# Attention inside a hybrid encoder layer: transposes, rounding and products with v one unit later

## The chip, the cores and the metric

The kernel runs on one core of a Trainium2 chip. Its engines work side by side, each through its own list of instructions in order: TensorE (PE in the profile; PEld is its weight load, which overlaps), VectorE (DVE), ScalarE (ACT), GpSimd (POOL) and SyncE (SP), of which the last two here mainly issue DMAs. Instructions of different engines wait for each other through semaphores. TensorE writes its results to PSUM, which the kernel uses as eight banks of 128 x 512 float32 values; a bank is taken, filled by TensorE, read by VectorE or ScalarE, and given back.

The metric is the device time of one launch in microseconds, as the median of several runs; less is better.

## What is computed

One layer: an RMS norm, one projection `w_in`, softmax attention in 16 heads of 64 beside gated linear attention in 4 heads, one projection `w_out`, then an RMS norm and a gated feed-forward part. There are 512 tokens, 2048 features, all in float32. The change lies in the softmax attention:

```python
def dilated_window_attention(q, k, v, rel_table, window, dilation):
    ...
    logits = (jnp.einsum('bhrnqd,bhrnkd->bhrnqk', qb, kb).astype(jnp.float32)
              * (Dh ** -0.5) + bias[None, :, None, None])
    logits = jnp.where(valid[None, None, None], logits, -1e30)
    m = jnp.max(logits, axis=-1, keepdims=True)
    p = jnp.exp(logits - m)
    s = jnp.sum(p, axis=-1, keepdims=True)
    o = jnp.einsum('bhrnqk,bhrnkd->bhrnqd', p, vb.astype(jnp.float32)) / s
...
def mixture_of_dilations(q, k, v, rel_table):
    for window, dilation in DILATION_PATTERNS:
        o, l = dilated_window_attention(q, k, v, rel_table, window, dilation)
    ...
    w = jax.nn.softmax(jnp.stack(lses, axis=0), axis=0)
    out = sum(w[i][..., None] * outs[i] for i in range(len(outs)))
```

The kernel folds the three dilation patterns into one table of biases per head and computes one softmax over 512 keys.

## The kernel before

**Precision.** TensorE's fast float32 form rounds its inputs. Each operand is therefore split into a rounded part and what is left over ("hi" and "lo"), and a product takes three matmuls (hi x hi, hi x lo, lo x hi), or two where one side needs no split. Rounding is a ScalarE copy, the rest a VectorE subtraction; both show in the profile under their lines (L237 and L218 for streamed weights, L671 and L677 for the softmax).

**Jobs.** Between about 400 and 750 us TensorE works through jobs of dense matmuls, each run by `run_job` (L308): gqk, gv0 and gv1 (projections for the gated attention), then out(1), out(2), ... for `w_out`. A job fills four banks; its inner loop issues groups of three matmuls (L346 to L348), one group for each bank and slice of rows. At its end the four banks are emptied by the job's evacuation: L836 and L839 on VectorE for gqk, L861 on ScalarE for gv0 and gv1, L1298 on VectorE for the out jobs. The banks go back one by one to a list from which the next `ps.get()` takes the one that was given back first.

**Side work.** Between two groups, `run_job` adds a quarter of the job's rate to a credit, 3.1 for gqk and the gv jobs and 4.0 for the out jobs. For every whole credit `run_side` takes one step from the front of a list of urgent generators (if there is one) and one from the front of the side list: the low-rank gate, then `attention()`, then the `silu` gates and `gla`, the gated attention with four heads in `turns`. A generator's step reaches to its next `yield`. All order on the engines follows from these lists, and the engines' instructions stand in the order in which the Python code issues them.

**Attention.** It has 64 units: 16 heads times 4 blocks of 128 queries. A step of `attention()` (L720 on) handles several units at different stages and has two halves with a `yield` behind each. In step u before the change:

- first half: scores of unit u on TensorE (`att_scores`, L631 and L632, into a bank); scale of unit u - 2 (`att_scale`, L658, ScalarE, odd units only); exp of u - 1 (`att_exp`, L649, ScalarE); rounding of u - 3 (`att_round`, L671, ScalarE); in even steps the lift (`att_lift`, L697, ScalarE) of a pair of units;
- second half: transposes of u - 2 (`att_transpose`, L663, TensorE, into a bank); in odd steps the products with v (`att_av`, L687 and L688, TensorE, into a bank); then on VectorE the rest of u - 3 (`att_rest`, L677, which frees the transposes' bank), the maximum with bias of u (`att_max`, L641, which frees the scores' bank), in even steps the mix of a pair (`att_mix`, L706, which frees the products' bank), and the reciprocal of the sum of u - 1 (`att_norm`, L652), with the normalisation of even units right behind it (L654).

Scaling by the reciprocal thus falls to ScalarE for odd units and to VectorE for even ones. The job holds four banks, attention has the other four.

**What feeds it.** q and k of a pair of heads are read back from memory by `read_qk` (L569, DMAs on GpSimd) in steps with u % 8 == 2 and rounded by `load_qk` (L588 on VectorE, L592 on ScalarE, five stages) which is put into the urgent list in steps with u % 8 == 5, so that one stage is issued ahead of each half step. `load_bias` (L552, a DMA on SyncE) reads the bias tables of two heads ahead at the first block of a head; `load_v` reads the second half of v in steps 33 to 35.

**Gated attention.** `gla` issues its gates, a scan (L950) and its tables (L962 to L981, VectorE, with exp on ScalarE between), then some empty half steps, and then transposes of keys (L1016) and products (L1019), each into a bank of its own, which `copy_predicated` (L1022) and a copy (L1026) empty. Head 0 has one more empty half step than the others.

Of the kernel before, what the change touches and what calls it, by code (L numbers as in the profile page):

```python
# [27 lines left out]
NH = 16  # L28
# [84 lines left out]
def put(*slots):  # L113
    for s in slots:
        if s.home is not None:
            s.home.free.append(s.i)


def layer(nc, tc, x, attn_norm_w, w_in, rel_table, gw_f, gb_f, gw_b, gb_b, gla_norm_w, w_out,
# [7 lines left out]
    with tc.manual_schedule(), \  # L127
# [134 lines left out]
        urgent = deque()  # L262

        def run_urgent():
            while urgent:
                try:
                    next(urgent[0])
                    break
                except StopIteration:
                    urgent.popleft()  # L270
# [277 lines left out]
        def load_bias(h):  # L548
            if h < NH and h not in biast:
                biast[h] = s4.get(F32, [P, BIASW])  # L550
                src = bass.AP(tensor=line.tensor, offset=line.offset + h * LINE, ap=[[1, P], [1, BIASW]])
                sp.dma_start(out=biast[h].t, in_=src)  # L552
# [18 lines left out]
        def load_qk(pr):  # L571


            qs, ks = qkr.pop(pr)
            sign = (-1.0, 1.0)[pr % 2]
            QK[pr] = []
            v = lambda x_: x_.rearrange("p (b c) -> p b c", c=P)
            low = slice(64, 128)
            todo = []
            for n in range(2):  # L580
                e, k = s2.get(F32R), s2.get(F32R)
                todo += [(v(e.t), v(e.f), v(qs[n].f)[:, :, ::-1], v(e.t)[low], -sign * DH ** -0.5, low, qs[n]),
                         (k.t, k.f, ks[n].f, ks[n].t, sign, slice(0, 128), None)]
                QK[pr].append((e, k, ks[n]))
            for m in range(5):
                if m:
                    _, hf, src, lo, scale, r, done = todo[m - 1]
                    dve.scalar_tensor_tensor(lo, src[r], scale, hf[r], op0=OP.mult, op1=OP.subtract)  # L588
                    if done:
                        put(done)  # L590
                if m < 4:
                    act.activation(todo[m][0], todo[m][2], AF.Copy, scale=todo[m][4])  # L592
                    yield
            ready.add(pr)

        def load_v(half, ts=range(4)):
            for t in ts:
                v = s4.get(F32R, [P, 8, 2, DH])
                VS.setdefault(half, []).append(v)
                sp.dma_start(out=v.f.rearrange("p h s c -> p (h s c)"), in_=vd[4 * half + t])  # L600
# [20 lines left out]
        UNITS = 4 * NH  # L621

        def att_scores(u):
            h, b = divmod(u, 4)
            q, k, kl = QK[h // 2][h % 2]
            c = slice(b * P, (b + 1) * P)
            if b == 0:
                load_bias(h)
                load_bias(h + 1)
            s = ps.get()  # L630
            mm(s.t, q.t[:, c], k.t, start=True, stop=False)  # L631
            mm(s.t, q.t[:, c], kl.t, start=False, stop=True)  # L632
            if b == 3:
                put(q, k, kl)
            AT[u] = s
# [77 lines left out]
        def attention():  # L713


            def run(f, u, n=UNITS):
                if 0 <= u < n:
                    f(u)

            for u in range(UNITS + 6):  # L720
                h = u // 4
                if u < UNITS:
                    if u % 8 == 2:
                        read_qk(h // 2 + 1)
                    if u % 8 == 5 and h // 2 + 1 < NH // 2:
                        urgent.append(load_qk(h // 2 + 1))
                    while h // 2 not in ready:
                        run_urgent()
                if "mix" in at:
                    pr = at.pop("mix")  # L730
                    mixh[pr] = split_of(mixf.pop(pr), big=pr > 4)
                run(att_scores, u)
                run(att_scale, u - 2)
                run(att_exp, u - 1)
                run(att_round, u - 3)
                if u % 2 == 0:
                    run(att_lift, (u - 6) // 2, UNITS // 2)
                yield
                run(att_transpose, u - 2)
                if u % 2:  # L740
                    run(att_av, (u - 5) // 2, UNITS // 2)
                run(att_rest, u - 3)
                run(att_max, u)
                if u % 2 == 0:
                    run(att_mix, (u - 6) // 2, UNITS // 2)
                run(att_norm, u - 1)
                if 33 <= u < 36:
                    load_v(1, ((0,), (1,), (2, 3))[u - 33])
                if u == UNITS - 3:
                    load_gla(0)  # L750
                yield
# [17 lines left out]
        def slow(steps):  # L769
            for _ in steps:  # L770
                yield
                yield
# [139 lines left out]
        def gla(h):  # L912
# [86 lines left out]
                load_gv(h // 2)  # L999
            yield  # L1000
            yield
            if h == 0:
                yield
            put(gq.pop(h), gk.pop(h))
            if h == NG - 1:
# [1180 lines left out]
```

## Time and profile before

| | us |
|---|---|
| median of 3 runs (2187.22 to 2187.71) | 2187.63 |
| the profiled execution | 2190.26 |
| its span, first to last instruction | 2188.5 |
| busy PE in the span | 2158.2 (99%) |
| busy DVE | 1844.7 (84%) |
| busy ACT | 1232.7 (56%) |
| busy POOL | 361.2 (17%) |

The mean granted TensorE clock of the profiled execution is 0.997 of full speed. Busy times are sums over instructions of one engine. A wait is read as "engine, tile, line that waited <- engine, tile, line that released it", with the total in us, how often, and the longest. In a timeline the first two columns are the start and the duration of an instruction, or of several alike that were merged (x4), and a bracket at the end gives the idle time just before it and what ended it. Matmuls overlap, so that several durations in a row do not add up to the time that they take.

### The profile page before, as it was taken

The page shows a single profiled execution, that of the slowest core. Times are in us where ns is not written, and L with a number is a line of the kernel's source. Part 1 is how long each engine was busy: PE and PEld are TensorE (multiplying, and loading weights), DVE is VectorE, ACT ScalarE, POOL GpSimd, SP SyncE. Part 2 cuts the span into 40 slices and gives each one's busy share as a digit, 9 for nine tenths or more (in the row PEclk, how much of TensorE's full clock was granted, in tenths as well). Part 3 has the DMA queues.
Part 4 walks back from the last instruction along what each step waited for, and adds up shares of the span by engine and source line. Part 5 has one row for each costly group of instructions (what it writes and reads, how often), then busy time and mean ns, then how long its engine had stood idle before and what let it go on. Part 6 is the DMA issues. An engine that isn't in the chain of part 4 may idle for free.

```text
span 2188.5 us, 35086 instructions
## 1 busy us (share of the span) xinstructions
PE 2158.2 (99%) x12714; PEld 1897.5 (87%) x12714; DVE 1844.7 (84%) x3191; ACT 1232.7 (56%) x2246; POOL 361.2 (17%) x501
## 2 busy tenths in 40 slices
PE   9999999999999999999999999999999999999998
PEld 7888888777777888988888888888888899999987
DVE  6689998687767878899999999898998888888885
ACT  8455555577675545555555555555555655565562
POOL 0011212311111110022121221112211220021300
PEclk9999999999999999999999999999999999999999
DMA  6467778754564684376767767677776985576982
GB/s 200 143 170 185 173 185 198 222 140 145 173 222 136 239 279 145 107 186 173 182 182 182 192 173 184 183 183 188 178 183 181 262 204 174 181 190 155 282 310 77
DMA packets 265691, 407.55 MB, mean 186 GB/s; under 512 B 19309, under 2 KB 163613, under 8 KB 265518
## 3 DMA queue, kind: packets, MB, share of 16 engines
q1 hardware_dynamic: 206238, 274.59, 39.9%
q0 software_dynamic: 58960, 130.19, 26.7%
q8 instruction: 100, 1.64, 0.3%
q14 instruction: 73, 0.60, 0.1%
q10 hardware_dynamic: 320, 0.53, 0.1%
HBM read 287.47 MB, written 66.39 MB: 162 GB/s over the span
## 4 chain that ended last, share of the span: by engine, by line
PE 57%; DVE 0%; DMA 0%; issue 0%; ACT 0%; DVEq 0%; ACTq 0%
PE ps L1526 24%; PE ps L1512 12%; PE ps L1889 5%; PE ps L1888 5%; PE ps L1887 5%; PE ps L347 1%; PE ps L346 1%; PE ps L348 1%; PE ps L2084 1%; PE ps L2083 1%; PE ps L2082 1%; DMA gd<-b 0%; DVE b L1435 0%; DVE a L2115 0%; DVE a L1546 0%
## 5 line engine op out<-in xcount | busy, mean ns | idle before, releaser
L1430 ACT CAST b<-b 128x1024 fp32r<-128x1024 f32 (+1 forms) x585 | 533.8, 944 | 391.2 <-DVE b L1435 196.7
L1435 DVE TENSOR_TENSOR b<-b,b 128x1024 fp32r<-128x1024 f32 (+1 forms) x585 | 613.8, 1084 | 32.6 <-ACT b L1430 20.3
L1526 PE MATMUL ps<-b,b 128*128 128x512 f32 x1708 | 500.7, 393 | 0.4 <-ACT b L1430 0.2
L1526 PE MATMUL ps<-a,b 128*128 128x512 f32 x1428 | 418.8, 394 | 1.3 <-DVE b L1546 0.6
L1526 PEld LDWEIGHTS ps<-b,b 128*128 128x128 f32 x1708 | 289.5, 188 | 32.5 <-ACT b L1430 0.7
L1512 PEld LDWEIGHTS ps<-b,b 128*128 128x128 f32 x1708 | 280.6, 190 | 40.8
L1512 PE MATMUL ps<-b,b 128*128 128x256 f32 x1708 | 307.4, 280 | 0.0
L1512 PEld LDWEIGHTS ps<-a,b 128*128 128x128 f32 x1428 | 237.0, 189 | 38.2 <-DVE b L1435 0.7
L1526 PEld LDWEIGHTS ps<-a,b 128*128 128x128 f32 x1428 | 238.5, 188 | 25.2 <-ACT b L1430 1.8
L1512 PE MATMUL ps<-a,b 128*128 128x256 f32 x1428 | 256.6, 280 | 0.3 <-DVE b L1435 0.3
L1417 DVE TENSOR_TENSOR b<-b 128x512 f32<-128x512 f32 x268 | 183.3, 684 | 18.9 <-PE ps L1889 7.1
L1887 PE MATMUL ps<-b,b 128*128 128x256 f32 x624 | 176.6, 283 | 0.0
L1888 PE MATMUL ps<-b,b 128*128 128x256 f32 x624 | 176.6, 283 | 0.0
L1889 PE MATMUL ps<-b,b 128*128 128x256 f32 x624 | 176.6, 283 | 0.0
L346 PE MATMUL ps<-b,b 128*128 128x512 f32 x348 | 140.4, 404 | 0.0
L348 PE MATMUL ps<-b,b 128*128 128x512 f32 x348 | 136.3, 392 | 0.2 <-DVE b L459 0.2
L347 PE MATMUL ps<-b,b 128*128 128x512 f32 x348 | 136.2, 391 | 0.0
L1418 DVE TENSOR_TENSOR b<-b,b 128x256 f32<-128x256 f32 x268 | 114.0, 425 | 9.3
L1419 DVE TENSOR_TENSOR b<-b,b 128x256 f32<-128x256 f32 x268 | 113.9, 425 | 9.2
L1887 PEld LDWEIGHTS ps<-b,b 128*128 128x128 f32 x624 | 119.8, 192 | 0.0
L1888 PEld LDWEIGHTS ps<-b,b 128*128 128x128 f32 x624 | 119.8, 192 | 0.0
L1889 PEld LDWEIGHTS ps<-b,b 128*128 128x128 f32 x624 | 119.8, 192 | 0.0
(306 smaller groups left out, 4020.4 us busy)
## 6 DMA issues: line engine op xcount, KB each, us to landing
b<-in_w_gate_dram SPq DMA_DIRECT2D x109, 512.0 KB, 3.8
b<-in_w_up_dram SPq DMA_DIRECT2D x88, 512.0 KB, 3.7
b<-in_w_down_dram SPq DMA_DIRECT2D x88, 512.0 KB, 5.6
b<-in_w_in_dram SPq DMA_DIRECT2D x86, 512.0 KB, 3.9
b<-a POOLq DMA_DIRECT2D x168, 256.0 KB, 4.6
b<-in_w_out_dram SPq DMA_DIRECT2D x32, 512.0 KB, 5.7
gd<-b POOLq DMA_DIRECT2D x22, 512.0 KB, 4.0
b<-gd SPq DMA_DIRECT2D x22, 512.0 KB, 8.5
```

The source lines that it names most:

```text
L346: mm(o, xh.t[:, c], wh.t[:, w], start=first and not on, stop=False, skip_group_check=on)
L347: mm(o, xh.t[:, c], wl.t[:, w], start=False, stop=False, skip_group_check=on)
L348: mm(o, xl.t[:, c], wh.t[:, w], start=False, stop=last, skip_group_check=on)
L1417: dve.tensor_tensor(s_[:, :, 0:2], r[:, :, 1:3], r[:, :, 0:1].to_broadcast(shape), op=OP.add)
L1418: dve.tensor_tensor(s_[:, :, 2], s_[:, :, 0], r[:, :, 2], op=OP.add)
L1430: act.copy(o, src)
L1435: dve.tensor_tensor(o, src, h, op=OP.subtract)
L1512: mm(o, wl, xh, start=False, stop=end, skip_group_check=True)
L1526: mm(o.rearrange("p (s t) -> p s t", s=2), wh, x_, start=first and p == 0, stop=False, skip_group_check=True)
L1887: mm(o, xh[:, t], wh, start=first and h == 0, stop=False, skip_group_check=True)
L1888: mm(o, xh[:, t], wl, start=False, stop=False, skip_group_check=True)
L1889: mm(o, xl[:, t], wh, start=False, stop=last, skip_group_check=True)
```

## The change

The units' stages are set one unit further apart, and the parities of the pair steps change:

- transposes of u - 3 instead of u - 2; rounding and rest of u - 4 instead of u - 3;
- products with v in even steps instead of odd ones (pair (u - 6) / 2), lift and mix in odd steps instead of even ones (pair (u - 7) / 2), the loop one step longer;
- `read_qk` in steps with u % 8 == 1, `load_qk` in steps with u % 8 == 4 and wrapped in `slow`, so that it issues a stage in every second half step;
- `load_bias` reads one head at blocks 0 and 2 instead of two heads at block 0; the second half of v is read in steps 34 to 36;
- head 0 of `gla` has two more empty half steps than the others instead of one.

```diff
@@ att_scores
-            if b == 0:
-                load_bias(h)
-                load_bias(h + 1)
+            if b % 2 == 0:
+                load_bias(h + b // 2)
@@ attention
-            for u in range(UNITS + 6):
+            for u in range(UNITS + 7):
                 h = u // 4
                 if u < UNITS:
-                    if u % 8 == 2:
+                    if u % 8 == 1:
                         read_qk(h // 2 + 1)
-                    if u % 8 == 5 and h // 2 + 1 < NH // 2:
-                        urgent.append(load_qk(h // 2 + 1))
+                    if u % 8 == 4 and h // 2 + 1 < NH // 2:
+                        urgent.append(slow(load_qk(h // 2 + 1)))
...
                 run(att_scores, u)
                 run(att_scale, u - 2)
                 run(att_exp, u - 1)
-                run(att_round, u - 3)
+                run(att_round, u - 4)
+                if u % 2:
+                    run(att_lift, (u - 7) // 2, UNITS // 2)
+                yield
+                run(att_transpose, u - 3)
                 if u % 2 == 0:
-                    run(att_lift, (u - 6) // 2, UNITS // 2)
-                yield
-                run(att_transpose, u - 2)
+                    run(att_av, (u - 6) // 2, UNITS // 2)
+                run(att_rest, u - 4)
+                run(att_max, u)
                 if u % 2:
-                    run(att_av, (u - 5) // 2, UNITS // 2)
-                run(att_rest, u - 3)
-                run(att_max, u)
-                if u % 2 == 0:
-                    run(att_mix, (u - 6) // 2, UNITS // 2)
+                    run(att_mix, (u - 7) // 2, UNITS // 2)
                 run(att_norm, u - 1)
-                if 33 <= u < 36:
-                    load_v(1, ((0,), (1,), (2, 3))[u - 33])
+                if 34 <= u < 37:
+                    load_v(1, ((0,), (1,), (2, 3))[u - 34])
@@ gla
-            if h == 0:
+            for _ in range(2 if h == 0 else 0):
                 yield
```

```python
        def slow(steps):
            for _ in steps:
                yield
                yield
```

No engine has more or fewer instructions than before. In the rows below, ps, a and b are banks and slots with their numbers, the result stands left of the arrow, and lines behind L627 are one lower after the change (its code is one line shorter). First VectorE in a pair of steady steps, before:

```order
L677 TENSOR_TENSOR b28_537_5706<-ps0_246_5684,b6_536_5705 128x4x128
L641 ISA a1_325_5726,small_76<-ps6_247_5700,b12_522_5427 128x512
L641 ISA small_76 128x1
L652 RECIPROCAL small_76<-small_76 128x1
L654 TENSOR_SCALAR a25_324_5690<-a25_324_5690,small_76 128x512
L218 TENSOR_TENSOR b29_535_5695<-b32_520_5417,b29_535_5695 128x512
L677 TENSOR_TENSOR b28_537_5706<-ps2_248_5711,b6_536_5705 128x4x128
L641 ISA a16_327_5759,small_76<-ps0_250_5735,b9_529_5573 128x512
L641 ISA small_76 128x1
L706 TENSOR_TENSOR a14_310_5523<-ps7_249_5716,a10_326_5740 64x2x128
L652 RECIPROCAL small_76<-small_76 128x1
```

and after:

```order
L676 TENSOR_TENSOR b6_534_5658<-ps0_242_5637,b32_533_5657 128x4x128
L640 ISA a3_323_5681,small_76<-ps5_243_5653,b12_522_5483 128x512
L640 ISA small_76 128x1
L651 RECIPROCAL small_76<-small_76 128x1
L218 TENSOR_TENSOR b29_531_5632<-b19_516_5395,b29_531_5632 128x512
L676 TENSOR_TENSOR b6_534_5658<-ps4_244_5666,b32_533_5657 128x4x128
L640 ISA a7_327_5708,small_76<-ps0_246_5691,b12_522_5483 128x512
L640 ISA small_76 128x1
L705 TENSOR_TENSOR a26_313_5548<-ps2_245_5671,a19_326_5697 64x2x128
L651 RECIPROCAL small_76<-small_76 128x1
L653 TENSOR_SCALAR a3_323_5681<-a3_323_5681,small_76 128x512
```

The mix (64x2x128) has moved from the step without a normalisation (L654) to the step with one, ahead of its reciprocal. The reciprocal for which the next scale waits (that of an odd unit) stands right behind a maximum now.

The second place is TensorE where gv0 ends and gv1 begins. Before, gv0 fills ps7 last, and the bank ps6 for the transposes is emptied by the third of the job's four evacuations on ScalarE (the L861 that reads ps6_176):

```order
L346 MATMUL ps7_177_4705<-a1_301_5465,b1_59_669 128x512
L347 MATMUL ps7_177_4705<-a10_302_5466,b1_59_669 128x512
L348 MATMUL ps7_177_4705<-a1_301_5465,b1_59_669 128x512
L346 MATMUL ps4_239_5624<-b14_526_5529,b7_8_165 128x512
L347 MATMUL ps4_239_5624<-b14_526_5529,b7_8_165 128x512
L348 MATMUL ps4_239_5624<-b14_526_5529,b7_8_165 128x512
L663 MATMUL ps6_243_5637<-idn_71,a16_311_5566 128x128 x4
```

After:

```order
L346 MATMUL ps0_176_4691<-b14_521_5455,b1_59_669 128x512
L347 MATMUL ps0_176_4691<-b14_521_5455,b1_59_669 128x512
L348 MATMUL ps0_176_4691<-b14_521_5455,b1_59_669 128x512
L346 MATMUL ps1_238_5625<-a4_309_5518,b7_8_165 128x512
L347 MATMUL ps1_238_5625<-a23_310_5519,b7_8_165 128x512
L348 MATMUL ps1_238_5625<-a4_309_5518,b7_8_165 128x512
L662 MATMUL ps0_242_5637<-idn_71,a20_308_5512 128x128 x4
```

The transposes follow the same group of matmuls, and now take ps0, the bank that the job filled last and that the fourth evacuation empties.

The third place is TensorE at the start of out(2), whose four banks are numbered 310 to 313. Before, the transposes of the gated attention (L1016) come behind its first four groups, and take ps6, which out(1) held as ps6_304 and its evacuation (L1298) empties:

```order
L348 MATMUL ps2_313_6764<-b9_603_6589,a18_207_4542 128x512
L1016 MATMUL ps6_315_6788<-idn_71,a13_389_6691 128x128 x4
L1019 MATMUL ps7_314_6787<-a14_388_6690,a13_389_6691 128x128 x4
L346 MATMUL ps0_310_6761<-b1_606_6619,a31_239_4856 128x512
L347 MATMUL ps0_310_6761<-b1_606_6619,a31_239_4856 128x512
```

After (the three rows of each group stand here by their first):

```order
L348 MATMUL ps6_313_6767<-b1_599_6589,b30_477_4562 128x512
...
L346 MATMUL ps3_310_6764<-b32_603_6618,b17_491_4882 128x512
...
L346 MATMUL ps7_311_6765<-b32_603_6618,b17_491_4882 128x512
...
L346 MATMUL ps2_312_6766<-b32_603_6618,b17_491_4882 128x512
...
L346 MATMUL ps6_313_6767<-b32_603_6618,b17_491_4882 128x512
...
L1015 MATMUL ps0_315_6811<-idn_71,a10_395_6706 128x128 x4
L1018 MATMUL ps4_314_6810<-a29_394_6705,a10_395_6706 128x128 x4
```

Four more groups of out(2), twelve matmuls, stand ahead of the transposes. Their bank ps0 was also out(1)'s (ps0_302).

## The prediction

> **What bounds the kernel now.** I began with busy time in windows of 402 to 750 us, where almost all of TensorE's idle time lies; these are the windows that hold it. Columns: window, its length, then busy us of PE, PEld, DVE, ACT and POOL with their instructions, the granted clock, the share of the DMA engines, GB/s.
>
> ```profile
> 402.00:450.00 48.00, 45.35 (x240) 36.70 (x238) 35.08 (x84) 33.23 (x71) 10.86 (x19) 1.00 0.53 150
> 450.00:500.00 50.00, 47.59 (x256) 38.48 (x256) 39.20 (x96) 33.68 (x73) 10.42 (x20) 1.00 0.50 138
> 500.00:541.00 41.00, 39.14 (x214) 31.94 (x214) 33.71 (x79) 30.82 (x66) 4.26 (x8) 1.00 0.56 162
> 541.00:550.00 9.00, 6.63 (x28) 5.15 (x27) 3.92 (x11) 6.41 (x14) 4.76 (x9) 0.81 0.54 167
> 550.00:600.00 50.00, 47.57 (x261) 38.75 (x259) 37.98 (x90) 35.66 (x76) 5.51 (x11) 1.00 0.55 163
> 600.00:620.00 20.00, 19.50 (x108) 15.72 (x107) 14.56 (x37) 13.32 (x30) 0.27 (x1) 1.00 0.41 139
> ...
> 655.00:666.00 11.00, 7.57 (x34) 6.43 (x33) 7.79 (x15) 3.69 (x9) 0.54 (x1) 0.69 0.21 81
> ```
>
> Length less busy PE, from 402 to 620: 2.65 + 2.41 + 1.86 + 2.37 + 2.43 + 0.50 = 12.2 us. This stretch is attention beside the matmuls of jobs gqk, gv0 and gv1. Two short windows lose clock as well: 9.0 x (1 - 0.81) = 1.7 us and 11.0 x (1 - 0.69) = 3.4 us. The stretch is bound by TensorE, then, less about 6% in which it waits; the change can win only such waits, since it removes no work. The waits of PE over the whole kernel say for whom (us in total, times, longest):
>
> ```profile
> PE ps L663 <- ACT a L658: 4.5, 12, 0.5
> PE ps L631 <- DVE b L677: 4.2, 6, 1.6
> PE ps L1016 <- DVE b L1298: 3.4, 1, 3.4
> PE ps L663 <- ACT b L861: 2.4, 1, 2.4
> ...
> PE ps L631 <- DVE a L836: 0.9, 1, 0.9
> PE ps L922 <- DVE b L1298: 0.9, 1, 0.9
> ```
>
> The transposes (L663) wait for the scaling of their unit (L658); the scores (L631) wait for a bank that the rest (L677) frees. The other four are single events where one job hands over to the next. Why the first two are late is read in one pair of steps, on ScalarE and then on VectorE (start, duration, instruction, idle time before it and its releaser):
>
> ```profile
> 479.59 0.72 ACT L658 ACTIVATE a<-a,small 128x512 f32<-128x512 f32 x1 [1.47 <-DVE small L652]
> 480.22 0.71 ACT L649 ACTIVATE a<-a,small 128x512 f32<-128x512 f32 x1
> ...
> 483.00 0.73 ACT L649 ACTIVATE a<-a,small 128x512 f32<-128x512 f32 x1 [0.84 <-DVE small L641]
> ...
> 486.11 0.72 ACT L658 ACTIVATE a<-a,small 128x512 f32<-128x512 f32 x1 [0.91 <-DVE small L652]
> ```
>
> ```profile
> 479.02 0.41 DVE L706 TENSOR_TENSOR a<-ps,a 64x256 f32<-64x256 f32 x1
> 479.35 0.15 DVE L652 RECIPROCAL small<-small 128x1 f32<-128x1 f32 x1
> ...
> 481.66 0.69 DVE L677 TENSOR_TENSOR b<-ps,b 128x512 fp32r<-128x512 f32 x1
> 482.27 0.68 DVE L641 CUSTOM_DVE_ANT_0 a<-ps,b 128x512 f32<-128x512 f32 x1
> ...
> 484.31 0.69 DVE L677 TENSOR_TENSOR b<-ps,b 128x512 fp32r<-128x512 f32 x1 [0.76 <-ACT b L671]
> 484.92 0.68 DVE L641 CUSTOM_DVE_ANT_0 a<-ps,b 128x512 f32<-128x512 f32 x1
> ```
>
> Scale, exp, round on ScalarE, then rest, max (and in every second step mix and reciprocal) on VectorE, then scale again: a ring, and it takes 486.11 - 479.59 = 6.52 us for two units. TensorE without its waits needs (218 - 12.2 - 1.7) / 32 = 6.4 us for two units (32 pairs between 402 and 620). The ring is the slower by about 0.1, and that is why both kinds of wait keep coming back.
>
> **The change, part by part.** Every engine keeps its instructions and their counts; only their places move, so each term is a wait that goes or comes.
>
> *Transposes a unit later.* The scale of a unit then stands a whole step (half of 6.8 us, 218 / 32) ahead of its transposes, against a wait of at most 0.5 now. All 12 waits go: **-4.5**. Neither scale, exp nor reciprocal is shortened; if scale falls a full step behind for other reasons, this is 0.
>
> *Mix and lift out of the ring.* The product moves to even steps, lift and mix to odd ones, where the scale of that step already lies behind. The reciprocal for which the next scale waits then follows max directly: 479.35 - 479.02 = 0.33 less, a ring of some 6.2 against TensorE's 6.4. The waits of the scores for the rest should shrink, with 0 left as one bound. The other: the odd step now carries mix (0.41), and the normalisation, between max and the next rest, so one foreign operation there, as long as a step of rest to max (482.27 - 481.66 = 0.61), makes the next rest late, and the even step has the product on TensorE between transposes and scores; then all 4.2 stay and the transposes' 4.5 may join them. With a slack of 0.2 for disturbances of 0.6 I leave most of it, 3.0 of 4.2: **-1.2**.
>
> *Reading and rounding q and k.* Spread over every second step it adds no instruction and puts one stage, not two, between neighbouring rounds; its reads start a step earlier and are used as many steps later. The stages take the idle of 0.76 ahead of the even rest. 0, already in the 3.0.
>
> *Bias a head at a time.* Its issue moves from four units ahead of the first max that needs it to two, 6.8 us. Landing:
>
> ```profile
> L552 SPq EVENT_SEMAPHORE  x20: 17/28/11727, 381.6 to 576.9; - x20
> ...
> DMA to landing us min/median/max: 3.4/3.6/5.2
> ```
>
> The longest landing leaves 1.6 us; I take 0. The semaphore row shows why that may fail (a rival below).
>
> *First handover, gqk to gv0.* The scores that took the bank of the second evacuation (0.9 us for L836) now take that of the third, with the job's evacuation starting earlier: bounds -0.9 and +0.7, **+0.2** taken.
>
> *Second handover, gv0 to gv1.* From the timeline:
>
> ```profile
> 542.33 2.43 ACT L861 ACTIVATE b<-ps,small 128x512 f32<-128x512 f32 x4
> ...
> 544.24 0.66 PE L663 MATMUL ps<-idn,a 128*128 128x128 f32 x4 [2.37 <-ACT b L861]
> ```
>
> Four evacuations take 2.43, one each 0.61. Now the transposes take the bank of the third; after the change, by the order, that of the fourth. The gap is then 2.9 to 3.0: **+0.6**. The bounds are -2.4 (an earlier evacuation and no gap) and +0.6 + 1.7 (a second stretch at half clock beside the one there is).
>
> The clock's loss of 1.7 in this window stands behind a gap of 2.37 and nothing longer. [...]
>
> *Third handover, out(1) to out(2).* First TensorE, then VectorE:
>
> ```profile
> 655.03 0.39 PE L347 MATMUL ps<-b,a 128*128 128x512 f32 x1
> 655.26 0.39 PE L348 MATMUL ps<-b,a 128*128 128x512 f32 x1
> 659.08 1.12 PE L1016 MATMUL ps<-idn,a 128*128 128x128 f32 x4 [3.43 <-DVE b L1298]
> ```
>
> ```profile
> 657.75 2.47 DVE L1298 TENSOR_TENSOR b<-b,ps 128x512 f32<-128x512 f32 x4
> ```
>
> The transposes of the gated scan (L1016) come behind the first four groups of out(2) and wait for the evacuation of out(1), which VectorE begins 2.1 us after even those groups end (655.26 + 0.39), behind the scan's tables. The extra half-step of gla's head 0 and the longer attention put the transposes twelve matmuls further back, 12 x (655.26 - 655.03) = 2.8 us that run inside the old gap. VectorE's tables also slide, by 0 to 1.4. So the gap is 3.43 - 2.8 + 0.9 = 1.5: -1.9. A gap of 1.6 (the longest of the scores' six, in the first window) lost no clock, as the 1.00 there shows, so the 3.4 of clock goes too. Against it, the second group of transposes now takes a bank that the first group has just used, and waits for VectorE and ScalarE to empty it: +0.9 (one evacuation of 0.6 and the start of it). Together **-4.4**, between 0 (tables and transposes slide alike) and -6.8 (no gap, no new wait).
>
> *Behind it* the wait at L922 (0.9) and another small one shift by some matmuls: **+0.3**, between -0.9 and +1.5.
>
> Sum: -4.5 - 1.2 + 0.2 + 0.6 - 4.4 + 0.3 = -9.0. The profiled execution took 2190.26 (its span 2188.5, the rest lies around it), 2.6 above the median of the runs, 2187.63; I carry the difference over: 2187.63 - 9.0 = **2178.6 us**.
>
> **Rivals.** *The ring stays the bound.* The rest's lateness is not cured and every transpose wait becomes a wait of the scores on L677. For it: VectorE is busy 37.98 of 50 us, and the odd step gets longer. Against: mix leaves the path. Then -4.5 + 4.5 in attention: 0.2 + 0.6 - 4.4 + 0.3 = -3.3, 2184.3.
>
> *The third handover keeps its gap*, because the scan's tables slide as far as the transposes: -9.0 + 4.4, 2183.0. For it: the evacuation is held by VectorE, not by TensorE. Against: the tables were waiting for ScalarE just before, so they need not slide in full.
>
> *All waits go*: -4.5 - 4.2 - 6.8 and a little of the handovers, 2171. For it: TensorE's 6.4 exceeds the new ring. Against: foreign operations on VectorE arrive unevenly.
>
> *Slower: the bias comes late.* SyncE issues in order; at L552 it has waited up to 11.7 us in the semaphore row. With two units' notice, max is late as soon as that wait exceeds 6.8 - 3.6 = 3.2 us, and behind max stand reciprocal, normalisation, and rest, then the scores. If 7 of the 15 loads come 2 us late, that is +14 - 9 = +5, 2192.6. Against: the slot it takes is free some units ahead by the order, and the median wait is 28 ns.
>
> **How the numbers follow.** Chances: forecast 0.54, ring 0.16, third handover 0.11, all waits gone 0.11, bias late 0.08. A measurement of this kernel tells 0.2% (4.4 us) from no change: faster is below 2183.25, slower above 2192.0. Faster takes the forecast, the case of no waits, half of the third handover and a quarter of the ring: 0.54 + 0.11 + 0.05 + 0.04 = 0.74; same has the rest of those two, 0.18; slower the bias, 0.08. The range, 2170 to 2187, runs from the case without waits to the ring with a worse second handover (2184.3 + 1.7) and leaves out mainly the bias; the forecast's own is 2174 to 2182.
>
> **What would show it.** In the waits of PE: no L663 behind L658; the scores behind L677 with some 3 us in total; L663 behind L861 with 2.9; L1016 behind L1298 near 1.5, and the window around it at clock 1.00. A ring that still binds would show as L631 waits of 5 us or more, in even steps. Late bias would show as VectorE's max waiting for a DMA. I am wrong if the windows from 402 to 620 lose as much as 12 us, or if a handover drops the clock a second time.

## The result and the profile after

The changed kernel takes **2181.88 us** in the median of 9 runs (2179.69 to 2184.24) against 2187.63 of 9 runs before (2186.10 to 2192.21). The ratio is 0.9973, 95% interval 0.9963 to 0.9984: 5.75 us less, or 0.26%. The forecast was 2178.6 in a range of 2170 to 2187.

The profiled execution has a span of 2180.2 us, against 2188.5. Not all of these 8.3 us belong to the change: the first matmul of job gqk starts 1.8 us earlier already (377.77 against 379.55 us), in code that is the same. From there to the first matmul of the next stage (786.80 against 795.07) the stretch is 409.0 us long instead of 415.5: -6.5.

The same windows as before, of the changed kernel (window, length, busy PE, PEld, DVE, ACT and POOL, granted clock, DMA share, GB/s):

```profile
402.00:450.00 48.00, 45.26 (x231) 36.93 (x230) 34.16 (x82) 31.86 (x68) 10.62 (x19) 0.96 0.49 146
450.00:500.00 50.00, 48.92 (x266) 40.01 (x266) 39.98 (x97) 36.52 (x79) 10.46 (x20) 1.00 0.51 143
500.00:541.00 41.00, 37.44 (x205) 30.52 (x203) 32.53 (x78) 31.63 (x67) 8.77 (x17) 1.00 0.60 188
541.00:550.00 9.00, 8.67 (x41) 7.21 (x42) 1.96 (x5) 4.26 (x10) 0.54 (x1) 0.81 0.46 158
550.00:600.00 50.00, 47.22 (x257) 38.26 (x256) 39.30 (x95) 36.58 (x79) 5.27 (x10) 1.00 0.52 166
600.00:620.00 20.00, 20.00 (x118) 17.11 (x117) 14.88 (x37) 14.69 (x34) 0.00 (x0) 1.00 0.24 82
...
655.00:666.00 11.00, 10.26 (x56) 8.74 (x57) 10.57 (x20) 6.99 (x13) 2.55 (x5) 1.00 0.59 188
```

Length less busy PE from 402 to 620 is now 10.5 us (12.2 before), so attention has won little. The window at 655 has won 2.7 us of idle time and all of its clock. But the first window shows a clock of 0.96: a stretch at half clock that was not there before. It lasts from 423.21 to 426.62 us and so costs half of 3.41, 1.7 us. The waits of PE:

```profile
PE ps L630 <- DVE b L676: 5.9, 6, 2.4
PE ps L662 <- ACT b L860: 2.8, 1, 2.8
PE ps L1015 <- DVE b L1297: 1.6, 1, 1.6
...
PE ps L630 <- DVE a L838: 0.9, 1, 0.9
...
PE ps L1018 <- DVE a L1021: 0.5, 1, 0.5
```

The wait of the transposes for the scale is gone altogether. The wait of the scores for the rest has grown from 4.2 to 5.9, and its longest case from 1.6 to 2.4 us. That longest case is at 422 us. VectorE ahead of it (start, duration, instruction):

```profile
417.90 0.49 DVE L653 TENSOR_SCALAR a<-a,small 128x512 f32<-128x512 f32 x1
418.30 0.68 DVE L588 SCALAR_TENSOR_TENSOR a<-a,a 128x512 fp32r<-128x512 f32 x1
418.90 1.22 DVE L1672 TENSOR_TENSOR b<-b,a 128x1024 f32<-128x1024 f32 x1
420.04 0.68 DVE L218 TENSOR_TENSOR a<-b,a 128x512 fp32r<-128x512 f32 x1
420.75 0.69 DVE L588 SCALAR_TENSOR_TENSOR a<-a,a 64x512 fp32r<-64x512 f32 x1
421.47 0.69 DVE L676 TENSOR_TENSOR b<-ps,b 128x512 fp32r<-128x512 f32 x1
```

The rest (L676) starts 3.2 us after the first of four operations that do not belong to the softmax of this step: two roundings of q and k (L588), the scaling of the last piece of q and k by the front stage (L1672, 1.22 us) and a rest of streamed weights (L218). VectorE is never idle there. It falls in an even step, right behind the normalisation (L653); the first mix comes only at 426 us.

The kernel before has the same pile at the same place, one rounding longer, and TensorE waited 1.56 us behind it:

```profile
417.73 1.40 DVE L588 SCALAR_TENSOR_TENSOR a<-a,a 64x512 fp32r<-64x512 f32 x2
419.04 1.22 DVE L1673 TENSOR_TENSOR b<-b,a 128x1024 f32<-128x1024 f32 x1
...
421.61 0.69 DVE L677 TENSOR_TENSOR b<-ps,b 128x512 fp32r<-128x512 f32 x1
```

So the pile alone does not make 2.4 us. What is new ahead of it is a wait of VectorE in attention's third step: the maximum (L640) of the third unit waits for a DMA that reads one of the 512-column buffers (a):

```profile
408.98 0.69 DVE L640 CUSTOM_DVE_ANT_0 a<-ps,b 128x512 f32<-128x512 f32 x1 [4.40 <-DMA b<-a]
```

Before, this maximum had waited 0.6 us, for its scores.

### The profile page after: what moved, and what is told of

It is laid out like the page before. It is cut to its first block, busy times and chain, and to the rows that moved or that the text cites. A ratio compares the mean times of both kernels' runs of the same rounds, so it can differ in the third digit from the quotient of the medians.

```text
span 2180.2 us, 35076 instructions
## 1 busy us (share of the span) xinstructions
PE 2154.8 (99%) x12714; PEld 1897.6 (87%) x12714; DVE 1843.7 (85%) x3191; ACT 1233.1 (57%) x2246; POOL 360.6 (17%) x501
## 4 chain that ended last, share of the span: by engine, by line
PE 88%; DVE 5%; ACT 3%; issue 2%; DMA 2%; POOL 0%; DVEq 0%; ACTq 0%; POOLq 0%
PE ps L1525 32%; PE ps L1511 16%; PE ps L346 5%; PE ps L347 5%; PE ps L348 5%; PE ps L1887 5%; PE ps L1888 5%; PE ps L1886 5%; DMA b<-a 1%; DVE a L640 1%; DVE b L676 1%; PE ps L2083 1%; PE ps L2081 1%; PE ps L2082 1%; ACT a L648 1%
## 5 line engine op out<-in xcount | busy, mean ns | idle before, releaser
L1525 PE MATMUL ps<-b,b 128*128 128x512 f32 x1708 | 501.0, 393 | 0.4 <-ACT b L1429 0.2
L346 PE MATMUL ps<-b,b 128*128 128x512 f32 x340 | 137.6, 405 | 0.0
L348 PE MATMUL ps<-b,b 128*128 128x512 f32 x340 | 132.9, 391 | 0.0
L347 PE MATMUL ps<-b,b 128*128 128x512 f32 x340 | 132.8, 391 | 0.0
```

Of the source, the lines that this page charges most:

```text
L346: mm(o, xh.t[:, c], wh.t[:, w], start=first and not on, stop=False, skip_group_check=on)
L347: mm(o, xh.t[:, c], wl.t[:, w], start=False, stop=False, skip_group_check=on)
L348: mm(o, xl.t[:, c], wh.t[:, w], start=False, stop=last, skip_group_check=on)
L1525: mm(o.rearrange("p (s t) -> p s t", s=2), wh, x_, start=first and p == 0, stop=False, skip_group_check=True)
```

## The experiments

All times are medians with the kernel before run beside them; the kernel before gave 2187.6 to 2188.2 in these series.

**The third handover alone.** The kernel before, with

```diff
-            for u in range(UNITS + 6):
+            for u in range(UNITS + 7):
...
-            if h == 0:
+            for _ in range(2 if h == 0 else 0):
                 yield
```

> The kernel before with two edits only: one empty step at the end of attention and one more empty half step in gla's head 0, so that the transposes of the gated attention stand exactly where they stand in the changed kernel. Theory (the third handover is a matter of position alone): L1016 behind L1298 falls from 3.4 to about 1.6, the half clock there (3.4) goes, some 0.5 of new wait: -4.8, that is 2182 to 2184, and the waits of attention stay as before (L663 behind L658 4.5, L631 behind L677 4.2). Rival (the tables slide with the transposes, and the gain came from attention): L1016 stays near 3.4 and the time within 1 us of 2187.6.

Measured: 2185.65, ratio 0.9988 (0.9979 to 0.9997), a smaller gain than the theory had. The waits of PE of this kernel:

```profile
PE ps L663 <- ACT a L658: 4.4, 12, 0.5
PE ps L631 <- DVE b L677: 4.3, 6, 1.6
PE ps L663 <- ACT b L861: 2.4, 1, 2.4
...
PE ps L1016 <- DVE b L1298: 0.9, 1, 0.9
PE ps L1019 <- DVE a L1022: 0.5, 1, 0.5
```

Attention's waits are those of before to a tenth, L1016's wait has fallen from 3.4 to 0.9, and the half clock behind it is gone (the granted clock of the span is 0.998, before it was 0.997). So the handover follows from the position of the transposes, without any change in attention; in the profiled execution it brings 3.8 us from 380 us to the next stage (411.7 against 415.5), in the medians 2.6. What the change gains beyond this, 0.15% or some 3 us by the two ratios, is left for attention and the first two handovers. It is a rough figure, since each ratio is known to about 0.1%.

**The parities.** The changed kernel with products in odd steps, lift and mix in even ones, and the loop of attention one step longer:

```diff
-                if u % 2:
-                    run(att_lift, (u - 7) // 2, UNITS // 2)
+                if u % 2 == 0:
+                    run(att_lift, (u - 8) // 2, UNITS // 2)
...
-                if u % 2 == 0:
-                    run(att_av, (u - 6) // 2, UNITS // 2)
+                if u % 2:
+                    run(att_av, (u - 7) // 2, UNITS // 2)
...
-                if u % 2:
-                    run(att_mix, (u - 7) // 2, UNITS // 2)
+                if u % 2 == 0:
+                    run(att_mix, (u - 8) // 2, UNITS // 2)
```

> The changed kernel with the parities of before: products with v in odd steps, lift and mix in even steps, so another step later; transposes, rounding and rest stay one unit later. Theory (mix ahead of the reciprocal lengthens the ring): no waits of L662 behind L657, but the scores behind the rest 7.5 to 10 in total against 5.9, attention 2 to 4 us slower. Rival (depth alone did it, parity is worth nothing): the scores behind the rest 4 to 6, attention within 1 us of the changed kernel. The first handovers may fall otherwise, since all that follows attention is a step later.

Measured: 2189.47, ratio 1.0007 (0.9998 to 1.0015). The scores wait 4.3 us for the rest, as the rival had it, but the transposes now wait 2.7 us for the rest too, so 7.0 in all: neither theory had the wait change places. Most of the loss lies behind attention: two gaps of 2.0 and 2.3 us at 665 and 694 us that the changed kernel does not have. The second try takes out the extra half steps of `gla`, so that the gated attention stands where it stands in the changed kernel:

> The kernel of e2 with no extra empty half steps in gla's head 0, so that the transposes of the gated attention stand at the same place as in the changed kernel. Theory (e2 lost some 5 us to its handovers behind attention, and the parity itself about 1): idle time of TensorE from 402 to 655 us some 11.7 as in e2 against 10.5, L1015 behind L1297 near 1.6 again, no gaps of 2 us at 665 and 694: 2182.5 to 2184. Rival (the parity costs all of it): 2188 or more, with the third handover as in the changed kernel.

Measured: 2187.25 (2183.81 to 2190.03), ratio 0.9995 (0.9986 to 1.0004). This lies between the two expectations. The gaps at 665 and 694 are gone, but L1013 behind L1295 (the same transposes and evacuation) has 2.6, not 1.6, and the stretch from the first matmul of gqk to the next stage is 2.1 us longer in this profile than in the changed kernel's. From 402 to 655 us TensorE's waits add up to 11.2 us against 9.8. (The 10.5 us in the expectation is the idle time from 402 to 620; from 402 to 655 the changed kernel is idle for 11.8 us, e2 for 11.7 and e5 for 12.5.) The median lies 5.4 above the changed kernel's. The profiled execution was the shortest of its 11 runs and has only one stretch at half clock, with three gaps of 2.4 to 2.8 us; that a gap of this length cost clock in one profiled execution and none in another is shown in the last section. So this profile gives the parity some 1 us in attention (0.7 by idle time, 1.4 by waits), and the idle time of e2 gives it nothing; that the rest of the 5.4 is clock was not shown.

**The spread of q and k.** Reading and rounding as before the change:

```diff
-                    if u % 8 == 1:
+                    if u % 8 == 2:
                         read_qk(h // 2 + 1)
-                    if u % 8 == 4 and h // 2 + 1 < NH // 2:
-                        urgent.append(slow(load_qk(h // 2 + 1)))
+                    if u % 8 == 5 and h // 2 + 1 < NH // 2:
+                        urgent.append(load_qk(h // 2 + 1))
```

> The changed kernel with q and k read and rounded as before (read at u % 8 == 2, rounded from u % 8 == 5 in four half steps in a row). Theory (foreign work on VectorE between maximum and rest makes the scores wait, and spreading it relieves them): scores behind the rest 8 or more against 5.9, time 2183.5 to 2186. Rival (spreading is worth nothing): 5 to 6.5 and a time within 1 us of 2181.9.

Measured: 2184.28, ratio 0.9983 (0.9974 to 0.9992), with `PE ps L630 <- DVE b L676` at 9.8 us in 11 waits. The theory holds: the part that was priced at nothing takes 3.9 us of waits away, and without it the deeper transposes would have moved their 4.5 us into the scores' waits and more.

**The pile at 422 us.** The front's late scaling is issued three half pieces later:

```diff
-            if i == 9:
+            if i == 12:
                 fr.late()
```

> The changed kernel with the late scaling of the last pair of q and k (the 1.22 us operation on VectorE, L1672) issued three half pieces of the job later, where no rounding of q and k runs. Theory (it is this operation on top of two roundings and a rest of weights that makes the gap of 2.44 at 422 us and the half clock behind it): the gap falls to 1.2 or less, no half clock at 423, -3 us: 2178 to 2179.5. Rival (the roundings alone fill the odd step): a gap of 1.5 or more stays, 2181 to 2182.

Measured: 2179.74, ratio 0.9965 (0.9951 to 0.9978). The gap falls to 1.3, between the two expectations, but a second one of 0.8 follows one step later, and the scores' waits are 6.4 in total, no less than 5.9. What is won is clock: nothing between 10 and 2170 us is at half clock in this profile (granted clock 0.999, in the changed kernel's 0.997). Of the changed kernel's two stretches one went with the gap at 422; the other stood behind the gap of 2.83 at the second handover, which is still there but costs no clock in this execution (last section).

The operation made the gap long, but not by itself. In the six kernels that have it in its old place and whose third unit's maximum waits 3.5 to 5.0 us (the changed kernel, e2, e5, e6, e7, e9) the gap is 2.4 to 2.5 us. With that maximum on time and the operation in its old place it is 1.6, 1.6 and 1.1 (before, e1, e3); with the maximum late and the operation moved it is 1.15 to 1.32 (e4, e8, e10, e11). Both are needed. Up to that maximum e3 differs from the changed kernel only in that q and k are read a step later, so the earlier reads make it late. In e3 half of the reads wait for such a DMA instead (1.46 us on GpSimd). Which buffer is handed to whom was not traced.

**The other pile.** A like order of operations, without the late scaling, stands ahead of the wait of 1.15 us at 562 us in the changed kernel (timeline of VectorE):

```profile
558.76 0.49 DVE L653 TENSOR_SCALAR a<-a,small 128x512 f32<-128x512 f32 x1
559.17 0.68 DVE L588 SCALAR_TENSOR_TENSOR a<-a,a 128x512 fp32r<-128x512 f32 x1
559.77 0.69 DVE L218 TENSOR_TENSOR a<-b,a 128x512 fp32r<-128x512 f32 x1
560.37 0.69 DVE L410 TENSOR_TENSOR b<-a,b 128x512 fp32r<-128x512 f32 x1
561.09 0.69 DVE L588 SCALAR_TENSOR_TENSOR a<-a,a 64x512 fp32r<-64x512 f32 x1
561.81 0.69 DVE L676 TENSOR_TENSOR b<-ps,b 128x512 fp32r<-128x512 f32 x1
```

Behind the normalisation stands the rounding of the mixed heads (L410). The waits at 506 and 593 us (0.7 and 0.8) have it in the step ahead of theirs; the rest that ends them waits 0.7 us for ScalarE's rounding, which comes late through the reciprocal and the scale of that step. The rounding of the mixed heads comes once in eight steps; the edit holds it back by one step:

```diff
-                if "mix" in at:
+                if "mix" in at and (u % 2 or u > UNITS):
```

> The changed kernel with the rounding of the mixed heads (L409 on ScalarE, L410 on VectorE) held back from step u % 8 == 6 to 7, away from the step that follows mix and normalisation. Theory (the remaining waits of the scores are foreign operations of VectorE piled on the step that already has mix and normalisation): the gap of 1.15 at 562 us falls below 0.6, the scores behind the rest fall from 5.9 to 4 to 5, 2180.5 to 2181.5. Rival (VectorE's total is what binds there, a pile moved is a wait moved): 5.5 to 6.5 in total, 2181.5 to 2182.5.

Measured: **2177.62**, ratio 0.9957 (0.9944 to 0.9969). The waits of PE from 395 to 655 us:

```profile
PE ps L630 <- DVE b L676: 3.1, 2, 2.4
PE ps L662 <- ACT b L860: 2.9, 1, 2.9
PE ps L339 <- DVE a L218: 1.0, 1, 1.0
```

Of six waits of the scores two are left, one of them the 2.4 at 422. The time is lower than even the theory had: the third handover's wait has fallen too (1.6 to 0.9), and the first one's (0.9 to 0.5). This is the timeline of VectorE for the step that had waited 1.15 us at 562:

```profile
556.89 0.68 DVE L218 TENSOR_TENSOR a<-b,a 128x512 fp32r<-128x512 f32 x1
557.61 0.69 DVE L588 SCALAR_TENSOR_TENSOR a<-a,a 64x512 fp32r<-64x512 f32 x1
558.33 0.69 DVE L676 TENSOR_TENSOR b<-ps,b 128x512 fp32r<-128x512 f32 x1
...
559.62 0.67 DVE L410 TENSOR_TENSOR b<-a,b 128x512 fp32r<-128x512 f32 x1
560.20 0.68 DVE L588 SCALAR_TENSOR_TENSOR a<-a,a 128x512 fp32r<-128x512 f32 x1
561.72 0.69 DVE L676 TENSOR_TENSOR b<-ps,b 128x512 fp32r<-128x512 f32 x1 [0.84 <-ACT b L670]
```

L410 stands in the other step now, where VectorE still has 0.84 us to spare before the next rest. The rival, that a pile moved is a wait moved, is wrong here: the odd step's rest waits for ScalarE's rounding in any case, and an operation put there is hidden.

**The second handover.** gv0 and gv1 are emptied by both engines:

```diff
-                    act.activation(v.t[:, t % 2], banks[t].t, AF.Copy, scale=rstd1[:, t:t + 1])
+                    if t % 2:
+                        dve.tensor_scalar(v.t[:, 1], banks[t].t, rstd1[:, t:t + 1], None, op0=OP.mult)
+                    else:
+                        act.activation(v.t[:, 0], banks[t].t, AF.Copy, scale=rstd1[:, t:t + 1])
```

> The changed kernel with the second and fourth evacuation of gv0 and gv1 on VectorE instead of ScalarE. Theory (the gap of 2.83 at the second handover is the queue of four evacuations behind rounding on ScalarE, and the half clock is that gap falling into one stretch of 3.413 us): the gap falls below 0.8, no half clock at 542 us, 2177 to 2179.5. Rival (VectorE is the tight engine here, its two evacuations push rest and maximum back): the scores behind the rest gain what the transposes lose, 2181 to 2183.

Measured: 2181.39, ratio 0.9971 (0.9961 to 0.9981), no gain that can be told. The gap of 2.83 is gone (0.2 and 0.3 are left), as the theory had it, and a gap of 2.2 of the scores behind the rest comes at 548 us, as the rival had it, but not for the rival's reason. The half clock now follows that gap (548.88 to 552.29 us; granted clock of the span 0.998). ScalarE and VectorE of this kernel at that place:

```profile
544.15 0.59 ACT L670 CAST b<-ps 128x512 fp32r<-128x512 f32 x1 [1.60 <-DMA gvd<-b]
```

```profile
547.12 0.69 DVE L676 TENSOR_TENSOR b<-ps,b 128x512 fp32r<-128x512 f32 x1 [4.59 <-DMA gvd<-b]
```

Rounding and rest of the next pair of units wait for the stores of gv0: they take the two large buffers that those stores have not read out yet. In the changed kernel the same wait is there, 6.2 us long on VectorE, and hidden behind the gap of 2.83.

**Together.** Late scaling, later rounding of the mixed heads and both engines for gv0 and gv1; then the same without the third edit:

> The changed kernel with three edits together: the late scaling three half pieces later (e4), gv0 and gv1 emptied by both engines (e6), the rounding of the mixed heads a step later (e7). Theory (their gains lie at different places and add): no gap above 1.6 us from 400 to 760 us, no half clock there, 2175 to 2177.5. Rival (attention's ring takes it back, as the waits of the scores): 2178.5 to 2180.

> e8 without its third edit: gv0 and gv1 are emptied by ScalarE alone, as in the changed kernel. Theory (in e8 the split only moved the second handover's wait to the scores, 2.3 at 545 us): 2174.5 to 2176.5, with L662 behind L860 near 2.9 and no 2.3 of the scores behind it. Rival (the split is worth its 2 us here, since attention has slack now): 2177 or more.

Measured: 2175.29, ratio 0.9944 (0.9931 to 0.9956), and 2176.36, ratio 0.9946 (0.9933 to 0.9959). Both times are as expected. The first has a gap of 2.3 at 545 us, which its expectation had ruled out, the second its L662 behind L860 with 2.9 us: one wait in place of the other, and the two kernels cannot be told apart. Last, the first of the two with small buffers for the stores:

```diff
-                    if t % 2 == 0:
-                        v = s4.get(F32, [P, 2, 512])
+                    v = s2.get()
...
-                    if t % 2:
-                        pool.dma_start(out=gvd[2 * pr + t // 2], in_=v.t.rearrange("p b c -> p (b c)"))
-                        put(v)
+                    pool.dma_start(out=gvd[2 * pr + t // 2][:, t % 2 * 512:(t % 2 + 1) * 512], in_=v.t)
+                    put(v)
```

> e8 with the results of gv0 and gv1 in four small buffers of the other kind, each with a store of its own, instead of two large ones. Theory (the wait of 2.3 of the scores at 545 us comes from rounding and rest of attention, which take the large buffers that the stores of gv0 have not yet released: ScalarE and VectorE there wait for that DMA): no wait of the rest for the store, the gap at 545 below 0.6, -2 us: 2172.5 to 2174. Rival (rest is late there for its own work): the gap stays above 1.5 and the time at 2175.

Measured: **2171.82**, ratio 0.9931 (0.9918 to 0.9944), 16 us less than before, 10 less than the changed kernel and somewhat less than the theory had. Its waits of PE:

```profile
PE ps L630 <- DVE b L676: 3.0, 4, 1.3
...
PE ps L1016 <- DVE b L1298: 0.9, 1, 0.9
PE ps L630 <- DVE a L838: 0.9, 1, 0.9
```

No wait at the second handover of more than 0.3, none of the rest for a store, and no half clock between 10 us and TensorE's last matmul, at 2161 us, in this profile (granted clock 0.999). The small buffers with ScalarE emptying the banks alone were not run.

**gla's extra half step.** The changed kernel with one, as before:

```diff
-            for _ in range(2 if h == 0 else 0):
+            if h == 0:
                 yield
```

> The changed kernel with one extra empty half step in gla's head 0, as before the change. The transposes of the gated attention then stand six matmuls earlier than in the changed kernel and six later than before. Theory (each half step of distance is taken off the wait for the evacuation of out(1)): L1015 behind L1297 rises from 1.6 to some 2.5, in the range where a half clock of 3.4 us can follow: +1 to +3, 2183 to 2185. Rival (the longer attention alone did it): 1.6 or less and 2181 to 2182.5.

Measured: 2182.33, ratio 0.9973 (0.9964 to 0.9983), not to be told from the changed kernel. L1015 behind L1297 rises to 3.0, more than the theory had, and a half clock follows it (654.97 to 658.38 us), but two of the small waits behind it (0.5 and 0.5, L1018 and L1040) go: the stretch from gqk to the next stage is 409.4 us against 409.0. The waits of this handover and behind it add up to 4.7 us before, 3.7 in this kernel and 3.3 in the changed one. So the longer attention takes 1.0 off the sum, and the extra half step mostly moves a wait within it. The half clock at the second handover is missing from this profile though the gap of 2.8 is there, so the clock of the two profiles cannot be compared.

## Why the prediction was right, and where its sum was off

Direction and range were right, and the forecast of -9.0 was too large by 3.3 against -5.75. By the medians both halves seem to have fallen short: e1 gives the third handover 2.6 us (interval 0.7 to 4.6) where the prediction had 4.4, and some 3.2 are left for all the rest where it had 4.6. Term by term, from the waits of the two profiled executions:

| term | predicted | measured |
|---|---|---|
| transposes behind scale (4.5) | -4.5 | -4.3 (0.2 behind the rest is new) |
| scores behind the rest (4.2 to 5.9) | -1.2 | +1.7 |
| half clock behind that wait, 422 us | 0 | +1.7 |
| first handover (0.9 to 0.9) | +0.2 | 0.0 |
| second handover (2.4 to 2.8), its clock | +0.6, the same | +0.5, the same |
| third handover (3.4 to 1.6, clock 3.4, new wait 0.5) | -4.4 | -4.8 |
| the small waits behind it | +0.3 | 0.0 |
| sum | -9.0 | -5.2 |

The stretch itself is 6.5 shorter; some 0.6 of the difference are the waits of attention's last transposes and products before the change (0.3 and 0.3), which are gone and which the prediction left out; the last 0.7 was not traced. That this sum of -5.2 lies so near the median's -5.75 is partly luck, since one execution's half clocks are in it.

**The step that failed** is "Mix and lift out of the ring", by its sign. It priced the ring at 6.2 us against TensorE's 6.4 and left 3.0 of 4.2. It named the danger, a foreign operation on VectorE between the mix and normalisation and the next rest, and then counted one of 0.6 us. The trace shows two to four there, because three generators come round and meet in the same step: the rounding of the mixed heads in the first half of step 6 of every eight, the rounding of q and k about once per step from 4 on (twice in the steps at 422 and 562 us), and the weights. An average over two steps cannot show that. e7 settles it for the waits from 500 us on: with one of these operations a step later, the scores' waits fall to 3.1, close to what the prediction had. It does not touch the gap at 422, which is 0.9 of the 1.7 in the table. The pile there was to be read in the trace before, ahead of the longest of the six waits.

**"Reading and rounding q and k ... 0, already in the 3.0"** was mis-sized as well: e3 shows 3.9 us more of waits without it. It has a price too: reading q and k a step earlier makes the maximum of the third unit wait 4.4 us, and with the late scaling this makes the gap at 422. The prediction's remark that the stages take the idle time ahead of the even rest is not how it came out: the even rest now follows the pile without a pause (422, 529 and 562 us, 3.8 of the 5.9), and it is the odd one that has idle time ahead of it.

**The transposes** did what was said. The rival "the ring stays the bound" was half true: of the 4.3 won there, the scores' waits took 1.7 and the clock behind them 1.7. The test that the prediction gave for it, scores' waits of 5 us or more in even steps, is met in size, but only 2.1 of the 5.9 fall in even steps. Its other sign, a loss of 12 us from 402 to 620 us, is not met by idle time (10.5); with the 1.7 of the new half clock it is just reached.

**The handovers** came out as the rows said: 2.83 for "2.9 to 3.0" at the second, 1.57 for 1.5 at the third with its clock back. e1 shows that the third needs nothing from attention. At the second the sum had counted no change of clock, and the clock is lost again as in the row of before (0.81 in both): in the 3.41 us ahead of its half clock TensorE was idle for 2.22 us before the change and for 2.07 after it. That the second handover lost clock in both profiles is luck, since the same gap of 2.8 us cost none in e4 and e9. A second stretch at half clock came after all, but at 422 us, where none was looked for.

**The bias** is not late: VectorE's only wait of a maximum for a DMA is `DVE a L640 <- DMA b<-a: 4.4, 1, 4.4`, in attention's third step, and the bias is read by another DMA (b<-line). PE does not wait at that place, but the delay is part of the gap at 422 us.

**The sum's base** was the profiled execution of 2190.26, carried over to the median. That execution also had a half clock of 6.8 us length at its third handover and was 1.8 us slower before the change begins.

## What to carry to other kernels

When work is moved by one step in a pipeline whose steps repeat with period 8, list what else falls on each of the eight steps on the tight engine, not only the work of an average pair: the place where three generators meet sets the wait. Ask of every read that is moved ahead whose buffer it takes. A wait that is gone should be followed through to the next resource that is late, here the rest, then the store that held its buffer; the second handover's edit gained nothing that could be told until the buffers behind it were changed. And in these profiles gaps on TensorE of 2.2 to 3.4 us could cost more than their length (1.7 us more behind the 2.44 at 422 us), so splitting a gap can pay although the waits add up to the same.

## What the runs showed of the hardware

TensorE's half clock stood behind gaps of TensorE, from 545.42 to 548.83 and from 658.06 to 664.89 us in the kernel before, from 423.21 to 426.62 and from 542.67 to 546.09 us in the changed kernel: three stretches of 3.41 us and one of 6.83. In the 3.41 us ahead of each, in this order, TensorE was idle for 2.22, 2.41, 2.42 and 2.07 us. The gap of 1.56 us at 422 us in the kernel before and the one of 1.57 us at the third handover of the changed kernel were followed by full clock. In the aligned parity kernel (e5) two stretches of 3.4 us with nearly the same work of TensorE came out differently; each stands here with the 3.4 us behind it:

```profile
539.06:542.48 3.42, 1.49 (x11) 1.33 (x12) 1.86 (x5) 3.42 (x7) 1.14 (x2) 1.00 0.21 85
542.48:545.89 3.41, 3.41 (x11) 2.74 (x10) 0.00 (x0) 0.26 (x2) 0.00 (x0) 0.50 0.82 289
```

```profile
655.12:658.53 3.41, 1.50 (x13) 1.50 (x14) 3.41 (x7) 2.23 (x6) 0.00 (x0) 1.00 0.30 105
658.53:661.94 3.41, 3.41 (x23) 2.98 (x22) 3.41 (x8) 1.40 (x3) 1.34 (x3) 1.00 0.08 31
```

With 1.49 us of busy PE half clock followed (0.50), with 1.50 it did not (1.00). (The ends of matmuls are modelled, so the last digit is not to be trusted.) What made the difference was not shown. Nor does the length of a gap alone tell. This is the gap of 2.83 at the second handover in the kernel with the late scaling moved (e4):

```profile
535.30:538.71 3.41, 2.01 (x9) 1.31 (x7) 1.97 (x5) 3.31 (x7) 0.00 (x0) 1.00 0.48 141
538.71:542.12 3.41, 1.98 (x11) 1.73 (x12) 0.75 (x3) 3.07 (x7) 1.10 (x2) 1.00 0.51 195
542.12:545.53 3.41, 3.41 (x23) 2.96 (x22) 1.96 (x5) 0.17 (x1) 0.00 (x0) 1.00 0.30 118
```

It is as long as in the changed kernel, with 1.4 us of idle time in each of the first two rows, and costs no clock. Of the 24 gaps of 2.0 to 3.4 us in the 13 profiles of this study 16 are followed by half clock and 8 are not. A gap of 2 to 3 us thus cost 1.7 us more in some executions and nothing in others, and this would spread the runs of kernels that have several (e5's 11 runs lie 6.2 us apart, e8's 5 runs 2.5); that the single runs differ for this reason was not shown, as only one execution of each was profiled. The stretch of 6.83 us in the profile before has 1.02 us of idle time in its first half (658.06 to 661.47 us); the three of 3.41 us have none. Whether such idle time is what keeps the half clock on stays open with one such case.
